# The rare-overflow branch of a mixture-of-experts layer moved from the middle of the layer to its end

## The chip, the cores and the metric

The kernel runs on one core of one Trainium2 chip. The metric is the device time of one execution in microseconds. Three timed runs of the kernel before gave 2019.69, 2011.02 and 2018.78 us, a median of 2018.78 us. One further execution was profiled.

## The reference

The model has 256 tokens of width 1024 and two blocks one after the other, each two layers deep. The change touches the first block alone. Each of its layers is attention (dilated in layer 0, stick-breaking in layer 1), a layer norm, a mixture of experts, and a layer norm again:

```python
scores = jax.nn.sigmoid(xt @ router_w)           # 256 x 16 experts
# per token: the best of 4 groups, in it the 2 best experts, gates that sum to 1
y[t] = sum over the 2 chosen e of gate[t, e] * (silu(x[t] @ w_gate[e]) * (x[t] @ w_up[e])) @ w_down[e]
x = layer_norm(x * DEEPNORM_ALPHA + y, ln2_g, ln2_b)
```

Any expert may in principle be chosen by any number of tokens. Here x @ w_gate and x @ w_up are 1024 to 256 columns, w_down is 256 to 1024 columns.

## The kernel before

The two token halves c = 0, 1 (128 rows each) are the lists x[0], x[1]. The mixture layer is the function moe.

Routing gives each token a rank within each of its experts. For the usual case each of the 16 experts gets 64 slots: P is a 0/1 matrix from tokens to slots, and gather(k, b, t) multiplies 128 columns of x by P on TensorE, in two parts of precision (four products per call). XT holds the gathered columns. A call gather(k, 0, ...) for k = 0 to 7 serves the first eight experts; the first two go to psB, the next six to psA (four buffers). Then up(n) multiplies the slots of a pair of experts with their gate and up weights, hidden and hidden_T make the activation, the down weights follow, and back returns the slots to the tokens. After every two pairs, add adds the sum into x[c] in VectorE; the last two pairs stay in PSUM in acc and are added at the end, after which layer_norm writes y. The second half's layer norm is kept back in self.rest, which the next layer calls (finish).

A slot number above 64 does not fit. For that case there is a branch: ci holds the largest number of tokens of an expert, values_load loads it into a register of all five engines' queues (line 921), and tc.If(rv > 64) (line 922) guards overflow, which computes all 16 experts densely for the tokens that did not fit. Each engine jumps over its own part of the body. A tile that the body reads or writes counts as used by it: whoever needs that buffer next waits for the engine of the body to be past the branch. What is traced behind the branch is issued behind it, and what is traced ahead of it, ahead of it; between two branches the order on each queue is laid out by a planner.

Before, the branch stands in the gather, between gather k = 1 and k = 2. The body writes its transposed x into the buffer of XT, and its weights pass through the ring "row".

Buffers: the ring "x" has four buffers of 128 x 1024 (new_x takes two), the ring "raw" four (weights as loaded, in all layers), XT one. Weights come from SP's queue. In the next layer each weight tile is split: ScalarE copies the high part (whi<-raw, line 240), VectorE subtracts (wlo, line 241). layer_norm first writes the statistics of its input into the first twelve columns of its output y (line 418), then scales and shifts (lines 424, 427). The next layer's first step after layer 0 is the transposition of x[0] (line 266) into xTh and xTl, after layer 1 the squares of the second block's norm (line 294).

Of the kernel before, what the change touches and what calls it, by code (L numbers as in the profile page):

```python
# [7 lines left out]
F32 = mybir.dt.float32  # L8
# [3 lines left out]
OP = mybir.AluOpType  # L12
# [3 lines left out]
ALPHA = float(4 ** 0.25)  # L16
# [153 lines left out]
class Net:  # L170
# [643 lines left out]
    def moe(self, x, l):  # L814


        nc, A = self.nc, self.A
        v, tt, stt, act = nc.vector, nc.vector.tensor_tensor, nc.vector.scalar_tensor_tensor, nc.scalar.activation
        with self.tc.tile_pool(name="moe", bufs=1) as sp, self.psum(512) as self.pa:
# [21 lines left out]

# [78 lines left out]

            rv = nc.values_load(ci[0:1, 0:1], min_val=0, max_val=256)
            with self.tc.If(rv > 64):
                self.overflow(x, l, rank, gt)

# [35 lines left out]
            def add(ns):  # L960
                for c in range(2):
                    acc = [self.psA() for _ in range(2)]
                    back(acc, c, ns, True, True)
                    for s, a in zip(self.halves, acc):
                        stt(out=x[c][:, s], in0=x[c][:, s], scalar=1.0 if ns[0] else ALPHA, in1=a, op0=OP.mult, op1=OP.add)

            p = up(0)
            for n in range(8):
# [26 lines left out]
            y, gb = self.new_x(), self.ln_rows(l, 1)  # L995
            for c in range(2):
                with self.tc.issue_after(self.end.ins) if c else ExitStack():
                    for s, a in zip(self.halves, acc[c]):
                        tt(out=x[c][:, s], in0=x[c][:, s], in1=a, op=OP.add)
                if c == 0:  # L1000
                    self.layer_norm(x[0], gb, y[0], True)
        self.rest = lambda: self.layer_norm(x[1], gb, y[1])
# [15 lines left out]
    def overflow(self, x, l, rank, gt):  # L1018
# [4 lines left out]
        XT = sp.tile([128, 8, 1024], F32, name="XTo", tag="XT")[:, :, :256]  # L1023
        for c in range(2):
            for k in range(0, 8, 4):
                t = self.psC()
                for j in range(4):
                    nc.tensor.transpose(t[:, j * 128:j * 128 + 128], x[c][:, (k + j) * 128:(k + j) * 128 + 128], self.ident)
                self.evac(XT[:, k:k + 4, c * 128:c * 128 + 128], t.rearrange("p (j s) -> p j s", j=4))
        y = self.acc()  # L1030

        def load(ap):
            for j in range(2):
                raw = self.row()
                nc.sync.dma_start(out=raw, in_=ap[:, j * 1024:j * 1024 + 1024])
                yield raw

        for e in range(16):
            p = [self.psC() for _ in range(2)]
            for b in range(2):  # L1040
                for j, w in enumerate(load(self.A["egu"][l, e, b])):
                    for i in range(2):
                        k = 4 * b + 2 * j + i
                        for c in range(2):
                            self.mm(p[c], XT[:, k, c * 128:c * 128 + 128], w[:, i * 512:i * 512 + 512], k == 0, k == 7)
            hs = [self.hidden(p[c], g2[:, c, e:e + 1]) for c in range(2)]
            hs = [self.hidden_T(h) for h in hs]
            for j, w in enumerate(load(self.A["edn"][l, e])):
                for c in range(2):
                    for i in range(2):  # L1050
                        self.mm(y[c][i], hs[c][:, j, :], w[:, self.halves[i]], e == 0 and j == 0, e == 15 and j == 1)
        for c in range(2):
            for s, a in zip(self.halves, y[c]):
                v.scalar_tensor_tensor(out=x[c][:, s], in0=a, scalar=1.0 / ALPHA, in1=x[c][:, s], op0=OP.mult, op1=OP.add)
# [689 lines left out]
```

## Time and profile before

| | us |
|---|---|
| median of three timed runs | 2018.78 |
| lowest, highest | 2011.02, 2019.69 |
| the profiled execution, its own time | 2027.7 |
| its span, first to last instruction | 2025.7 |
| TensorE busy | 1919.8 (95%) |
| VectorE busy | 1186.3 (59%) |
| ScalarE busy | 862.8 (43%) |

Times in the profile count from the start of the span. PE is TensorE's products, PEld its weight loads, DVE VectorE, ACT ScalarE, POOL GpSimd, SP SyncE; a name with q (PEq, SPq) is the queue of that engine. A row gives the work as out<-in by the names of the tiles. Waits stand in brackets: the idle time ahead and what ended it. The mixture layer of layer 0 runs from about 326 to 485 us, that of layer 1 from about 636 to 795 us. [...]

### The profile page before, as it was taken

The numbers are of one execution on the slowest core, as the hardware profiler recorded it, in microseconds if no ns is written. First come the engines' busy times: TensorE is split into PE (matmuls) and PEld (weight loads), VectorE is DVE, ScalarE is ACT, GpSimd is POOL, SyncE is SP. The second block draws the span as 40 slices with busy tenths as digits, with TensorE's granted clock in tenths as the row PEclk, the third lists the DMA queues.
The fourth block names the chain that finished last, engine by engine and source line by source line (L and its number), as shares of the span: only waits on it lengthen the run. The fifth ranks groups of instructions, "written<-read, shape, count | busy, mean of one in ns | idle before, by whom it ended". The sixth has DMA issues, their size and how long they took to land. (4 is left out here: it accounts for less than half of the span.)

```text
span 2025.7 us, 36997 instructions
## 1 busy us (share of the span) xinstructions
PE 1919.8 (95%) x14866; PEld 1622.0 (80%) x14866; DVE 1186.3 (59%) x2329; ACT 862.8 (43%) x1786; POOL 193.3 (10%) x225
## 2 busy tenths in 40 slices
PE   7999997997897997999999999999999999999998
PEld 7999996434885443899888988998999888888997
DVE  6778775125876124855576556555555675556554
ACT  5656552112662112544543335445544533235443
POOL 1323220000220000000021100000000030100000
PEclk9999998998998998999998999999999999899999
DMA  8345346795436796655532215555555532215553
GB/s 280 126 137 164 127 135 240 278 408 191 146 125 222 268 388 232 211 188 187 184 113 77 93 62 178 185 188 168 199 187 188 188 103 83 84 61 176 189 186 107
DMA packets 102516, 357.10 MB, mean 176 GB/s; under 512 B 11888, under 2 KB 15136, under 8 KB 102208
## 3 DMA queue, kind: packets, MB, share of 16 engines
q1 hardware_dynamic: 97584, 341.70, 49.1%
q10 hardware_dynamic: 4704, 12.81, 2.0%
q8 instruction: 120, 1.97, 0.4%
q14 instruction: 60, 0.49, 0.1%
q0 software_dynamic: 48, 0.13, 0.0%
HBM read 353.53 MB, written 1.07 MB: 175 GB/s over the span
## 5 line engine op out<-in xcount | busy, mean ns | idle before, releaser
L241 DVE TENSOR_TENSOR wlo<-raw,whi 128x512 fp32r<-128x512 f32 (+1 forms) x910 | 626.1, 715 | 384.0 <-ACT whi L240 380.1
L240 ACT ACTIVATE whi<-raw 128x512 fp32r<-128x512 f32 (+1 forms) x910 | 529.8, 616 | 592.3 <-issue 197.6
L245 PE MATMUL psB<-xTh,whi 128*128 128x256 f32 x1792 | 507.7, 283 | 12.3 <-ACT whi L240 8.3
L247 PE MATMUL psB<-xTh,wlo 128*128 128x256 f32 x1792 | 506.4, 283 | 0.2 <-DVE wlo L241 0.2
L246 PE MATMUL psB<-xTl,whi 128*128 128x256 f32 x1792 | 506.1, 282 | 0.4
L245 PEld LDWEIGHTS psB<-xTh,whi 128*128 128x128 f32 x1792 | 340.1, 190 | 18.1 <-ACT whi L240 9.8
L246 PEld LDWEIGHTS psB<-xTl,whi 128*128 128x128 f32 x1792 | 340.1, 190 | 5.4 <-DVE xTl L241 1.5
L247 PEld LDWEIGHTS psB<-xTh,wlo 128*128 128x128 f32 x1792 | 340.3, 190 | 1.4 <-DVE wlo L241 0.7
L247 PE MATMUL psA<-whi,hl 128*128 128x512 f32 x352 | 139.5, 396 | 0.0
L245 PE MATMUL psA<-whi,hh 128*128 128x512 f32 x352 | 139.4, 398 | 0.0
L246 PE MATMUL psA<-wlo,hh 128*128 128x512 f32 x352 | 138.7, 394 | 0.0
L245 PE MATMUL psA<-xTh,whi 128*128 128x256 f32 (+1 forms) x352 | 107.8, 307 | 0.3 <-ACT vt L536 0.2
L247 PE MATMUL psA<-xTh,wlo 128*128 128x256 f32 (+1 forms) x352 | 105.1, 299 | 0.0
L246 PE MATMUL psA<-xTl,whi 128*128 128x256 f32 (+1 forms) x352 | 103.6, 295 | 0.3 <-DVE xTl L241 0.3
L245 PE MATMUL psB<-whi,xTh 128*128 128x384 f32 (+2 forms) x256 | 90.3, 353 | 3.6 <-DVE qs L547 1.7
L247 PE MATMUL psB<-whi,xTl 128*128 128x384 f32 (+2 forms) x256 | 88.7, 347 | 0.4 <-DVE xTl L241 0.3
L246 PE MATMUL psB<-wlo,xTh 128*128 128x384 f32 (+2 forms) x256 | 88.5, 346 | 0.3 <-DVE wlo L241 0.3
L296 POOL TENSOR_TENSOR ss<-ss,mh 128x1 f32<-128x1 f32 x14 | 9.8, 702 | 785.5 <-DVE ss L295 780.8
L250 PE MATMUL psB<-raw,XT 128*64 128x512 f32 x288 | 83.5, 601 | 0.0
L247 PEld LDWEIGHTS psA<-whi,hl 128*128 128x128 f32 x352 | 66.0, 188 | 16.8 <-DVE hl L241 0.7
L246 PEld LDWEIGHTS psA<-wlo,hh 128*128 128x128 f32 x352 | 66.6, 189 | 12.6
L245 PEld LDWEIGHTS psA<-whi,hh 128*128 128x128 f32 x352 | 66.3, 188 | 12.8 <-ACT hh L240 0.9
(414 smaller groups left out, 3036.1 us busy)
## 6 DMA issues: line engine op xcount, KB each, us to landing
raw<-in_ffn1gu_dram SPq DMA_DIRECT2D x88, 512.0 KB, 3.8
raw<-in_ffn2gu_dram SPq DMA_DIRECT2D x88, 512.0 KB, 3.7
raw<-in_egu_dram SPq DMA_DIRECT2D x72, 512.0 KB, 9.9
wf<-in_egu_dram SPq DMA_DIRECT2D x56, 512.0 KB, 8.6
raw<-in_dqk_dram SPq DMA_DIRECT2D x46, 512.0 KB, 3.9
raw<-in_ffn1dn_dram SPq DMA_DIRECT2D x44, 512.0 KB, 3.6
raw<-in_ffn2dn_dram SPq DMA_DIRECT2D x44, 512.0 KB, 3.6
raw<-in_wb_dram SPq DMA_DIRECT2D x40, 512.0 KB, 3.7
```

Source lines behind the costliest of these rows:

```text
L240: self.hi = self.nc.scalar.activation(hi, src, AF.Copy)
L241: return (self.nc.gpsimd if pool else self.nc.vector).tensor_tensor(out=lo, in0=src, in1=hi.bitcast(F32), op=OP.subtract)
L245: mm(out, a[0], b[0], start=start, stop=False)
L246: mm(out, a[0], b[1], start=False, stop=False)
L247: mm(out, a[1], b[0], start=False, stop=stop)
L250: return self.nc.tensor.matmul(out, a, b, start=start, stop=stop)
L296: nc.gpsimd.tensor_tensor(out=ss[:, 3:4], in0=ss[:, 2:3], in1=self.mh[:, :1], op=OP.pow)
```

## The change

The branch moves from the gather to the end of the layer, behind the last product and ln_rows, ahead of the last addition. The register load stands behind the first up. Since the body must still read x at the end, the sums go into a new pair of buffers z instead of into x; y is taken behind the branch. The body works on one token half after the other, adds into z, and takes its weights through the ring "raw", twice as many loads as before.

```diff
             t0 = [gather(k, 0, self.psB()) for k in range(2)]
-
-            rv = nc.values_load(ci[0:1, 0:1], min_val=0, max_val=256)
-            with self.tc.If(rv > 64):
-                self.overflow(x, l, rank, gt)
-
             fetch(todo[len(homes):])
             XT = sp.tile([128, 8, 1024], F32, name="XT")
...
                     for s, a in zip(self.halves, acc):
-                        stt(out=x[c][:, s], in0=x[c][:, s], scalar=1.0 if ns[0] else ALPHA, in1=a, op0=OP.mult, op1=OP.add)
-
+                        if ns[0]:
+                            tt(out=z[c][:, s], in0=z[c][:, s], in1=a, op=OP.add)
+                        else:
+                            stt(out=z[c][:, s], in0=x[c][:, s], scalar=ALPHA, in1=a, op0=OP.mult, op1=OP.add)
+
+            z = self.new_x()
             p = up(0)
+            rv = nc.values_load(ci[0:1, 0:1], min_val=0, max_val=256)
             for n in range(8):
...
-            y, gb = self.new_x(), self.ln_rows(l, 1)
+            gb = self.ln_rows(l, 1)
+
+            with self.tc.If(rv > 64):
+                self.overflow(x, z, l, rank, gt)
+            y = self.new_x()
             for c in range(2):
                 with self.tc.issue_after(self.end.ins) if c else ExitStack():
                     for s, a in zip(self.halves, acc[c]):
-                        tt(out=x[c][:, s], in0=x[c][:, s], in1=a, op=OP.add)
+                        tt(out=z[c][:, s], in0=z[c][:, s], in1=a, op=OP.add)
                 if c == 0:
-                    self.layer_norm(x[0], gb, y[0], True)
-        self.rest = lambda: self.layer_norm(x[1], gb, y[1])
+                    self.layer_norm(z[0], gb, y[0], True)
+        self.rest = lambda: self.layer_norm(z[1], gb, y[1])
...
-    def overflow(self, x, l, rank, gt):
+    def overflow(self, x, z, l, rank, gt):
...
-        XT = sp.tile([128, 8, 1024], F32, name="XTo", tag="XT")[:, :, :256]
+        XT = sp.tile([128, 8, 1024], F32, name="XTo", tag="XT")
+        y = [self.psA() for _ in range(2)]
+
+        def load(ap):
+            for j in range(2):
+                raw = self.wp.tile([128, 1024], F32, name="raw", bufs=self.nraw)
+                nc.sync.dma_start(out=raw, in_=ap[:, j * 1024:j * 1024 + 1024])
+                yield raw
+
         for c in range(2):
+            xT = XT[:, :, c * 128:c * 128 + 128]
             for k in range(0, 8, 4):
                 t = self.psC()
                 for j in range(4):
                     nc.tensor.transpose(t[:, j * 128:j * 128 + 128], x[c][:, (k + j) * 128:(k + j) * 128 + 128], self.ident)
...
+            for e in range(16):
+                p = self.psC()
+                for b in range(2):
+                    for j, w in enumerate(load(self.A["egu"][l, e, b])):
+                        for i in range(2):
+                            k = 4 * b + 2 * j + i
+                            self.mm(p, xT[:, k, :], w[:, i * 512:i * 512 + 512], k == 0, k == 7)
+                hT = self.hidden_T(self.hidden(p, g2[:, c, e:e + 1]))
+                for j, w in enumerate(load(self.A["edn"][l, e])):
                     for i in range(2):
...
+                        self.mm(y[i], hT[:, j, :], w[:, self.halves[i]], e == 0 and j == 0, e == 15 and j == 1)
+            for s, a in zip(self.halves, y):
+                v.tensor_tensor(out=z[c][:, s], in0=z[c][:, s], in1=a, op=OP.add)
```

## Rows read from the trace of the kernel before

**Rows 1.** The page, part 1: busy time of an engine, share of the span, instructions.
```profile
PE 1919.8 (95%) x14866; PEld 1622.0 (80%) x14866; DVE 1186.3 (59%) x2329; ACT 862.8 (43%) x1786; POOL 193.3 (10%) x225
```

**Rows 2.** The branch's line, both layers: queue, operation, ns min/median/max; then who waited.
```profile
L922 PEldq COMPARE_BRANCH  x2: 6052/6070/6088, 340.7 to 650.5; - x2
...
L922 DVEq COMPARE_BRANCH  x2: 56/64/72, 342.8 to 652.5; - x2
...
  PE psA L250: 11.9, 2
  ACT XT L536: 10.6, 2
```

**Rows 3.** Timeline of the gather, layer 0: start, us, engine, work, [idle before, releaser].
```profile
340.09 1.05 PE L250 MATMUL psB<-P,xsl 128*128 128x512 f32 x2
...
346.96 0.77 PE L250 MATMUL psA<-P,xsh 128*128 128x512 f32 x1 [5.81 <-PEq L922]
...
354.73 1.94 PE L250 MATMUL psB<-raw,XT 128*64 128x512 f32 x8
```

**Rows 4.** The same, layer 1.
```profile
649.55 1.06 PE L250 MATMUL psB<-P,xsl 128*128 128x512 f32 x2
...
656.74 0.77 PE L250 MATMUL psA<-P,xsh 128*128 128x512 f32 x1 [6.13 <-PEq L922]
...
664.88 1.94 PE L250 MATMUL psB<-raw,XT 128*64 128x512 f32 x8
```

**Rows 5.** Stretches: length, busy time (and count) by engine, granted clock, DMA share, GB/s.
```profile
337.08:341.14 4.06, 4.06 (x8) 2.29 (x8) 3.78 (x9) 0.63 (x1) 0.00 (x0) 0.50 1.02 404
341.14:344.50 3.36, 0.01 (x1) 0.00 (x0) 1.95 (x4) 0.63 (x1) 0.00 (x0) 1.00 1.03 408
346.96:351.34 4.38, 4.38 (x10) 3.44 (x11) 1.28 (x2) 1.20 (x2) 0.00 (x0) 0.50 0.50 180
351.34:354.73 3.39, 3.39 (x15) 2.45 (x14) 0.80 (x2) 1.20 (x2) 0.00 (x0) 1.00 0.22 82
...
650.60:656.74 6.14, 0.01 (x2) 0.04 (x1) 1.95 (x4) 0.63 (x1) 0.00 (x0) 0.50 0.69 272
355.00:370.00 15.00, 15.00 (x80) 8.01 (x76) 1.79 (x5) 1.58 (x3) 0.00 (x0) 1.00 0.60 184
445.00:460.00 15.00, 13.69 (x64) 5.43 (x64) 2.51 (x5) 1.85 (x4) 0.00 (x0) 1.00 1.03 408
```

**Rows 6.** DMA queues from 340.7 to 344.1 us: packets, MB, share.
```profile
q1 hardware_dynamic: 381, 1.39, 102.0%
```

**Rows 7.** DMA queues from 344.1 to 345.4 us.
```profile
q8 instruction: 1, 0.02, 5.3%
```

**Rows 8.** The register load's line, both layers.
```profile
L921 PEldq TENSOR_LOAD <-ci x2: 314/400/487, 340.1 to 650.1; - x2
```

**Rows 9.** Timeline of the end of layer 0.
```profile
472.97 2.89 SPq L221 DMA_DIRECT2D raw<-in_sv_dram  x4
...
484.25 0.39 PE L250 MATMUL psB<-yel,PT 128*128 128x512 f32 x1
...
485.20 1.28 DVE L418 BATCH_NORM_STATS2 x<-x 128x6 f32<-128x512 f32 x2
...
485.70 2.69 ACT L240 ACTIVATE whi<-raw 128x512 fp32r<-128x512 f32 x5
...
489.94 1.94 PE L266 MATMUL psC<-c0t,x 128*128 128x128 f32 x8 [5.30 <-DVE x L427]
...
491.06 0.60 ACT L240 ACTIVATE xTh<-psC 128x512 fp32r<-128x512 f32 x1 [2.67 <-PE psC L266]
```

**Rows 10.** Timeline of the end of layer 1.
```profile
795.86 1.28 DVE L418 BATCH_NORM_STATS2 x<-x 128x6 f32<-128x512 f32 x2
...
800.48 0.63 ACT L294 ACTIVATE row<-x 128x512 f32<-128x512 f32 x1 [3.57 <-DVE x L427]
```

**Rows 11.** DMA issues from 470 to 500 us: KB each, median us to landing.
```profile
raw<-in_sv_dram SPq DMA_DIRECT2D x4, 512.0 KB, 5.8
```

More of the change, by code (lines that the diff above doesn't have):

```diff
@@ L1028, in overflow @@
                     nc.tensor.transpose(t[:, j * 128:j * 128 + 128], x[c][:, (k + j) * 128:(k + j) * 128 + 128], self.ident)
[L1029 to L1041, printed above, removed]
-                    for i in range(2):
[L1043 to L1054, printed above, removed]
+                self.evac(xT[:, k:k + 4, :], t.rearrange("p (j s) -> p j s", j=4))
+            for e in range(16):
[7 more added lines that the diff above has]
+                for j, w in enumerate(load(self.A["edn"][l, e])):
+                    for i in range(2):
+                        self.mm(y[i], hT[:, j, :], w[:, self.halves[i]], e == 0 and j == 0, e == 15 and j == 1)
+            for s, a in zip(self.halves, y):
+                v.tensor_tensor(out=z[c][:, s], in0=z[c][:, s], in1=a, op=OP.add)
     def second_consts(self, pool):
```

## Prediction

> **What bounds the kernel now.** I read the page first. TensorE is busy for 95% of the span [rows 1], so only time in which TensorE stands still, or runs at the lower clock, can be won or lost. Next I read the line of the branch, which runs twice, once a layer. The branch instruction takes 6.07 us on TensorE's queue and 0.06 us on VectorE's [rows 2], and both TensorE's products and ScalarE's copies of XT waited for TensorE's queue to come past it, 11.9 and 10.6 us for the two layers. The timeline of the gather shows the place: the last product before the branch ends at 340.09 + 1.05 = 341.14 us, the next starts at 346.96 [rows 3]; in layer 1 the hole is 6.13 us [rows 4]. [...] Last, the end of the layer: TensorE ends at 484.25 + 0.39 = 484.64 us, then stands for 5.30 us until the normalized x[0] is there to transpose [rows 9]. That is the hole into which the branch moves.
>
> **Removed: the stall in the gather.** The reader is to see that the branch body is not run (nothing of its tiles is in the trace); what costs is TensorE's own jump over it. Without it the 24 products of the six gathers left (k = 2 to 7, four each) follow at once. Their inputs are in time: VectorE's last work before the branch fits into the 1.95 us that it is busy in the stretch behind 341.14 [rows 5], and psA has four buffers. The lower bound of the gain is the hole alone, 5.8 and 6.1 us. The upper bound has all 24 products at the high clock: 24 x 0.23 = 5.5 us, so the first expert product starts at 341.14 + 5.5 = 346.6 instead of 354.73 us, 8.1 us sooner; in layer 1 (hole 650.60 to 656.74, then 664.88 [rows 4]) 656.1, 8.8 us sooner. In layer 0 the clock was already granted at 1.00 when TensorE stopped, after 4.06 us of products, and it fell only behind the idle stretch; in layer 1 it was still at 0.50 [rows 5]. So I take 7.6 near the upper end for layer 0, and 7.4, the middle, for layer 1: **gain 15.0 us** (11.9 to 16.9).
>
> **Moved: the register load.** It stands behind the first expert products now. On TensorE's queue it takes 0.40 us, and from its start (340.1) to the branch (340.7) pass 0.6 us [rows 2, 8]. TensorE's queue runs ahead of the array, so between 0 and 0.6 us a layer; I take 0.3, **loss 0.6 us**. On the other four queues the same load meets idle time. SP and POOL pass the branch too; SP no longer meets it with loads in flight, and its next weight loads had to wait for buffers at either place: nothing. The additions into z are of the size of those into x, on VectorE, which is busy for 1.79 of 15 us between 355 and 370 and for 2.51 of 15 between 445 and 460 [rows 5]: nothing; without that cover it would be tenths of a microsecond a layer. The two loads of ln_rows now stand before the branch on SP, where nothing waits for them until the layer norm.
>
> **Added: the branch at the end.** Here the stall is not simply covered by TensorE's 5.30 us hole, and that is the main step. Two chains start behind TensorE's passing. (1) The branch body reads x[c] with TensorE (transposes), and y = new_x() takes x's buffers, as the ring holds four and z holds two. The first write into y is the statistics of the layer norm, which go into y[:, :12]. So this VectorE instruction, 485.20 us before [rows 9], waits until TensorE is past the branch, as ScalarE's XT copies do now [rows 2]. Behind it stand the whole layer norm, the transposes and the next layer's first product. (2) The body's weights now lie in the raw ring, read by TensorE. The next layer's first four weight tiles, which SP issues at 472.97 us before [rows 9], wait for the same moment.
>
> How long is the jump there? Upper bound: the same instruction, 6.07 us. Lower bound: in the gather the one packet of TensorE's instruction queue does not lie between 340.7 and 344.1 us, where the weight loads fill 102% of the DMA engines [rows 6], but between 344.1 and 345.4 [rows 7], and TensorE goes on at 340.7 + 6.09 = 346.8. If the fetch began at once, 346.8 - 344.1 = 2.7 us would be left. At the end of the layer TensorE's jump meets idle DMA engines, as the weight loads of the next layer wait too. So the row is an upper end, but how much of the first 3.4 us was the load can't be read from it; I take the middle, 4.4 us. [...] The jump is issued some 0.44 us before the last product ends (340.7 against 341.14), so at 484.2 here; it is past at 488.6, and 0.17 us later (346.79 to 346.96) the waiting engine starts: 488.8 against 485.20, **3.6 us a layer, 7.2 us** (1.9 to 5.2 a layer, 3.8 to 10.4). Layer 1 has the same distance, its statistics start at 795.86 [rows 10].
>
> Chain (2) on top. A weight tile lands 5.8 us after its issue by the median [rows 11], the transposed x is ready for ScalarE 491.06 - 485.20 = 5.9 us after the statistics [rows 9]. ScalarE's queue is in order, and before, the eight copies of these tiles (five of them in 2.69 us, 0.54 each) stand ahead of xTh in layer 0 [rows 9], four ahead of the squares at 800.48 us in layer 1 [rows 10]. If none stands ahead any more, nothing is added. If all eight do, with the tiles 1.3 us apart (512 KB at 408 GB/s [rows 5]), xTh starts 5.8 + 3 x 1.3 + 1.1 = 10.8 us after the passing instead of 5.9, 4.9 us more. ScalarE's own loads of constants behind the layer's end (msb, c2t) now land among these tiles, within the same bounds. I take 1.5 a layer, between the ends but nearer the lower, since tile and xTh come due within a microsecond of each other (5.8 against 5.9) and VectorE's work on x[1] can fill what is lost: **3.0 us** (0 to 9.8).
>
> **Sum:** -15.0 + 0.6 + 7.2 + 3.0 = -4.2 us. The profiled execution took 2027.7 us for its span of 2025.7 and would take 2023.5; the three timed runs have a median of 2018.8, 9 us lower, so I forecast 2018.8 - 4.2 = **2014.6 us**. Bounds: -16.9 + 3.8 = -13.1, and -11.9 + 1.2 + 10.4 + 9.8 = +9.5 us.
>
> **Rivals.** (a) The cost at the end nearly vanishes: the jump takes its lower 2.7 us and the copies stand behind xTh: -15.0 + 0.6 + 3.8 = -10.6, 2008.2 us. For it speaks the packet that came only as the weight loads ebbed [rows 6, 7]; against it that layers 0 and 1 show nearly the same 6.09 and 6.05 us. (b) The jump is cheap altogether, as on VectorE, 0.06 us [rows 2], because its target happens to be at hand: TensorE is past before 485.20, only the late weights cost: about -14 us, 2005 us. The body on TensorE is as long as before, which speaks against it. [...] (c) Slower: ScalarE's in-order queue holds xTh behind all late copies, and the jump stays at 6.07: -15.0 + 0.6 + 10.4 + 9.8 = +5.8, 2024.6 us. It decides from 7.2 us a layer on, that is, from 3.6 us of waiting behind the passing. For it speaks the order of before, against it that the copies can be laid out anew, as the code behind the branch is now ordered by itself. (d) The gain is not had: the weight stream sets the end of the layer. From 445 to 460 us the DMA engines are full at 408 GB/s and TensorE is busy for 13.69 of 15 us [rows 5]. Then -0 + 10.8, 2029.6 us. Against it: from 355 to 370 us the DMA engines are busy for only 0.60, because buffers come free as TensorE uses them, so the stream starts sooner with TensorE.
>
> **Chances and range.** The forecast 0.48, (a) 0.25, (b) 0.07, (c) 0.13, (d) 0.07. A measurement tells about 0.5%, 10.1 us, from no change: below 2008.7 or above 2028.9 us. Faster: all of (b), half of (a), a tenth of the forecast, 0.25. Slower: most of (d), a fifth of (c), 0.07. The same: 0.68. The range reaches from (b) to (c), 2005 to 2024 us; the forecast's own is 2009 to 2020.
>
> **What the changed profile would show.** The branch on TensorE at the end of each layer with 3 to 6 us; no hole above 1 us in the gather, and the first expert product about 6 us behind the last product on psB, not 354.73 - 341.14 = 13.6 us. The statistics of the layer norm waiting for TensorE's queue at that line, about 3.6 us later against the last product than now, and the next layer's first raw loads issued right behind it. The prediction is wrong if the statistics start before TensorE is past, if the gather still waits, or if ScalarE stands for more than 4 us on a weight tile with the transposed x ready.

## Result and profile after

The changed kernel takes **2030.6 us** (median of 16 runs, 2020.6 to 2038.4) against 2018.6 us (16 runs, 2010.4 to 2025.4) on the same chip: ratio **1.0062 [1.0046, 1.0079]**, some 12 us slower. The forecast was 2014.6 us, with a range up to 2024.

The page, part 1: TensorE's work is what it was [rows 1].

```profile
PE 1919.0 (95%) x14866; PEld 1621.4 (80%) x14866; DVE 1187.1 (59%) x2329; ACT 862.6 (43%) x1786; POOL 192.9 (10%) x225
```

The branch's line, both layers (it is L996 now), and who waited for it, us in total and times.

```profile
L996 DVEq COMPARE_BRANCH  x2: 63/68/72, 481.8 to 794.4; - x2
L996 PEldq COMPARE_BRANCH  x2: 3539/3609/3679, 482.1 to 794.7; - x2
...
  PE psA L250: 7.8, 2
  DVE x L1002: 2.0, 2
```

The jump is at the end of the layer and lasts 3.5 and 3.7 us, against 6.05 and 6.09 in the gather [rows 2]. Next the timeline of the gather, both layers: the last product on psB and the first expert product.

```profile
341.24 1.06 PE L250 MATMUL psB<-P,xsl 128*128 128x512 f32 x2
...
347.23 1.94 PE L250 MATMUL psB<-raw,XT 128*64 128x512 f32 x8
...
654.68 1.05 PE L250 MATMUL psB<-P,xsl 128*128 128x512 f32 x2
...
660.93 1.94 PE L250 MATMUL psB<-raw,XT 128*64 128x512 f32 x8
```

The hole is gone. From the first gather product to the first expert product pass 10.0 and 10.3 us, 7.7 and 8.1 less than before [rows 3 to 5]: the forecast's 7.6 and 7.4, met. Of these stretches the granted clock tells as well (layer 0, before, then changed: length, busy time and count of PE, PEld, DVE, ACT and POOL, granted clock, DMA share, GB/s; in layer 1 0.58, then 0.72):

```profile
337.08:354.73 17.65, 11.84 (x32) 8.21 (x33) 7.81 (x15) 3.65 (x6) 0.00 (x0) 0.69 0.63 245
```

```profile
337.23:347.23 10.00, 10.00 (x32) 7.65 (x32) 7.54 (x15) 3.66 (x6) 0.00 (x0) 0.74 0.84 333
```

Now the end of layer 0.

```profile
481.73 0.40 PE L250 MATMUL psB<-yel,PT 128*128 128x512 f32 x1
482.60 0.69 DVE L1002 TENSOR_TENSOR x<-x,psA 128x512 f32<-128x512 f32 x1 [0.89 <-DVEq L996]
485.75 2.89 SPq L221 DMA_DIRECT2D raw<-in_sv_dram  x4
485.78 0.77 PE L250 MATMUL psA<-yel,PT 128*128 128x512 f32 x1 [3.65 <-PEq L996]
486.34 0.63 PE L250 MATMUL psB<-yel,PT 128*128 128x512 f32 x1
486.58 0.69 DVE L1002 TENSOR_TENSOR x<-x,psA 128x512 f32<-128x512 f32 x1 [3.30 <-PE psA L250]
...
487.19 1.28 DVE L418 BATCH_NORM_STATS2 x<-x 128x6 f32<-128x512 f32 x2
...
489.79 1.15 ACT L240 ACTIVATE whi<-raw 128x512 fp32r<-128x512 f32 x2 [8.92 <-DMA raw<-in_sv_dram]
...
491.03 1.94 PE L266 MATMUL psC<-c0t,x 128*128 128x128 f32 x8 [4.06 <-ACT whi L240]
...
492.80 0.58 ACT L240 ACTIVATE xTh<-psC 128x512 fp32r<-128x512 f32 x1
...
495.41 0.58 PE L245 MATMUL psB<-whi,xTh 128*128 128x256 f32 x1 [1.38 <-ACT whi L240]
```

Three things stand here. Two of the layer's own last products were laid behind the branch, so they, the second half of the last addition and the statistics wait for the jump; without it they would have ended near 482.6 and the statistics begun 0.56 us later as before [rows 9], at 483.2 instead of 487.19: 4.0 us late (4.5 in layer 1 by the same count). The next layer's loads are issued right behind the jump, at 485.75, not ahead of the last products as before (472.97, [rows 9]). ScalarE then stands for 8.92 us on the first of these tiles, and TensorE's second projection product 1.38 us for a high part. At the end of layer 1, where the 1442 KB of c2t are loaded at the same time, xTh stands behind a tile that is late:

```profile
799.98 1.28 DVE L418 BATCH_NORM_STATS2 x<-x 128x6 f32<-128x512 f32 x2
...
807.22 1.94 PE L266 MATMUL psC<-c0t,row 128*128 128x128 f32 x8 [7.45 <-ACT whi L240]
...
809.30 1.83 ACT L240 ACTIVATE whi<-raw 128x512 fp32r<-128x512 f32 x3 [2.12 <-DMA raw<-in_ffn1gu_dram]
...
811.03 1.06 ACT L240 ACTIVATE xTh<-psC 128x512 fp32r<-128x512 f32 x2
```

All this is the cost at the layer's end that the forecast put at 10.2 us. The surprise is between the two ends of the layer. From the first expert product to the layer's last product, before and then changed:

```profile
354.73:484.64 129.91, 126.57 (x545) 53.80 (x544) 29.62 (x53) 18.69 (x38) 0.00 (x0) 1.00 0.84 316
```

```profile
347.23:486.97 139.74, 131.16 (x545) 55.37 (x544) 30.28 (x53) 17.68 (x36) 0.00 (x0) 0.98 0.76 286
```

The same 545 products take 9.8 us more. Only 4.4 us of these are the jump and the two products behind it (486.97 against 482.6). The other 5.4 us of the 7.7 won in the gather were spent inside the layer, ahead of the branch.

### The profile page after: what moved, and what is told of

Same layout as the page of the kernel before. It is cut to its first block, busy times and chain, and to the rows that moved or that the text cites. A ratio compares the mean times of both kernels' runs of the same rounds, so it can differ in the third digit from the quotient of the medians.

```text
span 2028.8 us, 36976 instructions
## 1 busy us (share of the span) xinstructions
PE 1919.0 (95%) x14866; PEld 1621.4 (80%) x14866; DVE 1187.1 (59%) x2329; ACT 862.6 (43%) x1786; POOL 192.9 (10%) x225
## 4 chain that ended last, share of the span: by engine, by line
PE 53%; DVE 3%; ACT 1%; issue 1%; POOL 1%; DMA 0%; SPq 0%; DVEq 0%; POOLq 0%; ACTq 0%
PE psB L247 8%; PE psB L246 8%; PE psB L245 8%; PE psA L245 7%; PE psA L247 7%; PE psA L246 6%; PE psC L250 5%; PE psB L250 3%; DVE wlo L241 1%; DMA raw<-in_ffn1gu_dram 0%; PE psC L266 0%; DVE row L298 0%; ACT xTh L240 0%; ACT whi L240 0%; DVE xTl L241 0%
## 5 line engine op out<-in xcount | busy, mean ns | idle before, releaser
L245 PE MATMUL psB<-xTh,whi 128*128 128x256 f32 x1792 | 508.7, 284 | 10.8 <-ACT whi L240 8.1
L245 PEld LDWEIGHTS psB<-xTh,whi 128*128 128x128 f32 x1792 | 340.7, 190 | 16.6 <-ACT whi L240 9.0
L247 PEld LDWEIGHTS psA<-whi,hl 128*128 128x128 f32 x352 | 66.1, 188 | 16.3 <-DVE hl L241 0.7
L245 PEld LDWEIGHTS psA<-whi,hh 128*128 128x128 f32 x352 | 66.4, 189 | 12.5 <-ACT hh L240 0.9
```

The source lines that it names most:

```text
L245: mm(out, a[0], b[0], start=start, stop=False)
L247: mm(out, a[1], b[0], start=False, stop=stop)
```

## How to compare the runs

One execution is not enough here. The last 9176 products, from the end of the first feed-forward network (about 1000 us) to the end of the kernel, lie far behind everything that the change touches. They took 1007.0 us in a second profile of the kernel before (first fence) and 1018.6 in the changed kernel (second fence), and by the counts and by the busy times of the other engines they are the same work (length, busy time and count of PE, PEld, DVE, ACT and POOL, granted clock, DMA share, GB/s):

```profile
1000.90:2007.90 1007.00, 980.98 (x9176) 884.02 (x9176) 608.55 (x1224) 449.65 (x947) 71.07 (x100) 0.99 0.43 144
```

```profile
1004.80:2023.40 1018.60, 989.54 (x9176) 892.01 (x9176) 608.83 (x1224) 449.63 (x947) 71.24 (x100) 0.98 0.43 143
```

What differs is how long TensorE was granted half of its full speed (a granted 0.50 and not 1.00; the means are 0.99 and 0.98): PE's busy time grows with the length, by 8.6 us. So beside each median stands the mean over all runs of span times granted clock: the time that the execution would take at a granted 1.00 throughout if all of it went with the clock, "at full clock" below. It counts a microsecond at a granted 0.50 as half of one, waiting included, so it compares kernels and is no time that anyone measured. Its standard error is 0.6 to 1.4 us. It is 1965.2 us for the kernel before (114 runs, standard error 0.3; its medians on the chips used were 2018.6 to 2024.5). Ratios are against runs of the kernel before on the same chip.

| kernel | median us | ratio | clock | at full clock |
|---|---|---|---|---|
| changed | 2030.6 | 1.0062 [1.0046, 1.0079] | 0.9712 | 1970.2 |
| b_none | 2023.5 | 1.0020 [1.0001, 1.0040] | 0.9714 | 1963.8 |
| a_none | 2022.1 | 1.0000 [0.9976, 1.0024] | 0.9733 | 1964.9 |
| a_raw2 | 2025.5 | 1.0016 [0.9996, 1.0035] | 0.9736 | 1968.7 |
| a_pin | 2031.0 | 1.0055 [1.0034, 1.0076] | 0.9714 | 1971.5 |
| a_pin_raw2 | 2017.7 | 0.9977 [0.9955, 0.9999] | 0.9759 | 1968.2 |
| a_hide | 2012.5 | 0.9955 [0.9930, 0.9981] | 0.9769 | 1965.7 |
| a_mid | 2025.4 | 1.0029 [1.0005, 1.0052] | 0.9709 | 1965.3 |
| b_light | 1991.7 | 0.9867 [0.9819, 0.9914] | 0.9745 | 1938.9 |
| b_none_light | 1986.4 | 0.9823 [0.9775, 0.9871] | 0.9745 | 1933.0 |
| b_short | 2009.3 | 0.9938 [0.9915, 0.9962] | 0.9750 | 1958.5 |
| b_reg | 2010.3 | 0.9939 [0.9911, 0.9968] | 0.9738 | 1955.8 |
| b_none_reg | 2002.1 | 0.9921 [0.9893, 0.9949] | 0.9753 | 1952.2 |
| a_reg | 2018.2 | 0.9975 [0.9950, 1.0000] | 0.9731 | 1960.4 |
| a_hide_reg | 2002.9 | 0.9925 [0.9894, 0.9956] | 0.9761 | 1953.7 |

## Experiments

**No branch at all.** From the kernel before and from the changed one the same lines go.

```diff
-            rv = nc.values_load(ci[0:1, 0:1], min_val=0, max_val=256)
-            with self.tc.If(rv > 64):
-                self.overflow(...)
```

> The kernel before without the register load, the branch and the branch's body; all the rest as it was. What the stall at the gather is worth at most. Theory 1 (the expert weights' stream takes the gain back inside the layer): in the changed kernel the first expert product came 7.7 and 8.1 us earlier in the two layers, the last one only 2.1 and 4.6 us; so without any branch the kernel gains some 5 to 9 us and not more: 2010 to 2014 us, and the last expert product of the layers stands 2 to 5 us earlier than before though the first stands some 7 to 8 us earlier. Rival (the gain of the gather is kept and lost at the end of the layer alone): 15 us less, 2003 to 2005 us, with the last expert product 7 us earlier in each layer.

> The changed kernel without the register load, the branch and its body; the sums stay in the new buffers z. What is left of the change when nothing branches. If the other buffers cost nothing, the time is that of the kernel before without a branch, within 2 us. Theory 1 (the weights' stream): 2010 to 2014 us, that is 17 to 21 us less than the changed kernel, all of which the branch at the end of the layer then costs with what hangs on it. Rival (buffers cost): 3 us or more above the kernel before without a branch.

Measured: neither is faster than the kernel before (2023.5 and 2022.1 us). The first expert products come 7 to 9 us earlier, and a stop of 6 us a layer is gone, for nothing. The two agree within 1.1 us at full clock, so no cost of the buffers z shows, and the branch at the end costs the changed kernel 1970.2 - 1964.9 = 5.3 us at full clock, 1.0062 - 1.0000 or 12.5 us in time. This looked like theory 1, the weights' stream.

**Half of the weights' bytes**, with and without the branch (half of each expert weight is left out, the other half used twice).

```diff
-                    raws[e, i] += self.fetch(ap, ring=ring)
+                    raws[e, i] += self.fetch(ap[:, :512], ring=ring)
```

> The kernel before with half of each expert weight left out: of every load of 1024 columns only the first 512 are fetched, and the products use these twice, so instructions and branch stay as they are and the stream's bytes are halved. It is the partner of the next kernel, the same without a branch. Theory 1 (the weights' stream paces the later expert products): the stage from the first to the last expert product is shorter than the 120 us of the kernel before, by 10 to 25 us a layer, and the DMA engines are never full in it. Rival (TensorE's own work paces the stage): no more than 4 us a layer are gained.

> The kernel without a branch, with the same half of each expert weight left out. Theory 1: with the stream out of the way the 7 to 8 us that the first expert product comes earlier are kept to the last expert product, 6 to 8 us a layer, and the time is 12 to 16 us under that of its partner with the branch at the gather. Rival (the lead is lost to something other than the stream, the clock or the order on TensorE): the lead shrinks to 1 to 4 us as with full weights, and the two times differ by under 6 us.

Measured: 5.3 us between the two, 5.9 at full clock. The lead at the first expert product was itself only 5.3 and 5.2 us, since the jump had become shorter (below), and 3.6 and 5.2 us of it reached the layer's last product. At full clock the stage from the first expert product to the layer's last product is 121.2 us in all four layers. The lead is kept here, as theory 1 wants, though the difference of the two times is under 6 us, as its rival wants; and it proved less than it seemed to, since both kernels of this pair have the same order on TensorE, and the pair before had not. Against the kernel before, half of the bytes take 26 us off at full clock; the order on TensorE was laid anew there too, so this is not the stream's price alone.

**A short body.** The jump's target is brought nearer: the body does one expert of sixteen (b_short) or six (b_mid) and leaves out the rest; it is not run with these inputs.

```diff
-        for e in range(16):
+        for e in range(1):
```

> The kernel before with the branch's body cut from sixteen experts to one, 44 products instead of 464 on TensorE; the body is not run with these inputs. If the jump's length comes from the distance to its target, as the forecast took it, it falls from 6.05 us to under 0.3 us, and the hole in the gather to under 1 us; the time is then that of the kernel before without a branch, 2018 to 2025 us, no faster than before. Rival (a taken branch on TensorE always has to fetch while the DMA engines are full): 5 to 6.3 us as before.

> The same with six experts, 184 products on TensorE. If the distance decides, and there is a distance up to which the target is at hand, the jump is either under 0.3 us or 5 to 6.3 us, nothing between. Rival (the jump grows with what is skipped): 2 to 3 us.

Measured, the branch's line in the two:

```profile
L922 PEldq COMPARE_BRANCH  x2: 212/285/358, 338.8 to 648.7; - x2
```

```profile
L922 PEldq COMPARE_BRANCH  x2: 6059/6160/6262, 337.3 to 650.8; - x2
```

Over 44 products the jump takes 0.2 to 0.4 us, over 184 as long as over 464. So it is the far target that costs, and nothing between was seen. The second half of the expectation failed, and that turned the study: the hole shrank only to 2.75 us, since TensorE then waits for VectorE to pass,

```profile
342.00 0.79 PE L250 MATMUL psA<-P,xsh 128*128 128x512 f32 x1 [2.75 <-DVEq L922]
```

yet the kernel is **12.5 us faster** by its ratio (0.9938 [0.9915, 0.9962], four runs; 6.7 us at full clock), against 4 us slower with no branch (1.0020). The stop at the gather is worth something after all. The time from one round's first activation (ScalarE, line 779) to the next in layer 0 shows what differs:

| round after round, us | 1-2 | 2-3 | 3-4 | 4-5 | 5-6 | 6-7 | 7-8 |
|---|---|---|---|---|---|---|---|
| before | 12.0 | 12.3 | 11.4 | 15.9 | 22.0 | 12.5 | 20.1 |
| b_short | 11.9 | 12.3 | 11.4 | 15.9 | 22.0 | 12.5 | 20.1 |
| b_none | 11.9 | 12.3 | 12.5 | 18.6 | 22.4 | 12.8 | 20.1 |
| changed | 11.9 | 12.3 | 12.5 | 17.8 | 22.6 | 12.8 | 20.1 |

In b_short each round comes 2.8 us earlier against the gather and lasts as long; a stream at its limit would not allow that. From the first expert product to the layer's last one, b_short and then b_none:

```profile
350.12:479.99 129.87, 126.53 (x545) 53.77 (x544) 29.65 (x53) 18.67 (x38) 0.00 (x0) 1.00 0.84 316
```

```profile
345.08:481.08 136.00, 130.70 (x545) 54.97 (x544) 29.90 (x53) 17.65 (x36) 0.00 (x0) 0.99 0.83 309
```

The order of b_short's products on TensorE between the first and the last up product is that of the kernel before, instruction by instruction. Without the branch at the gather the tool that lays out the program orders these products anew. TensorE hardly waits for weights there: 0.4 us once in layer 0 of b_none and of the changed kernel, never in their layers 1. In the order as laid it is thus not the stream that lengthens the stage. In b_none's timeline of the fifth round, up products (psB) and down products of the round before (psA) alternate, and the up products end late:

```profile
411.25 0.33 PE L787 MATMUL psC<-c0t,eh 128*128 128x128 f32 x1
...
412.60 1.87 PE L250 MATMUL psB<-wf,XT 128*64 128x512 f32 x6
413.88 0.59 PE L250 MATMUL psA<-raw,ehT 128*64 128x512 f32 x1
...
415.17 1.45 PE L250 MATMUL psB<-wf,XT 128*64 128x512 f32 x5
416.45 2.75 PE L250 MATMUL psA<-raw,ehT 128*64 128x512 f32 x10
```

The order of the changed kernel is new in the same way, but not that of b_none product by product.

**A fixed order.** The down products of a round wait for the last up product of the next; nothing else changes. In the kernel without a branch, in the changed one, in the one with the mended end (a_hide, below), and in the kernel before.

```diff
-                hT = self.hidden_T(h)
-                y = ...; down products
+                with self.tc.issue_after(self.up.ins):   # last up product of round n + 1
+                    hT = self.hidden_T(h)
+                    y = ...; down products
```

> The kernel before without a branch, with the order on TensorE fixed: the down products of a round wait for the last up product of the next. Order theory: the fifth round lasts 16 us again and not 18.7, the last expert product comes 130 to 133 us after the first gather product and not 135 to 137, and the time falls from 2023.5 to 2012 to 2017 us. Rival (the weights' stream): TensorE waits for weights inside the up products instead, the last expert product stays at 135 to 137 us, and the time at 2020 to 2025 us.

> The changed kernel with the same fixed order, everything else as changed. Order theory: 3 to 5 us a layer come back, 2021 to 2025 us; the rest of the loss is the layer's end. Rival (the stream): 2029 to 2032 us as changed.

> The kernel with all three edits at the layer's end, and the fixed order. If both costs of the change are taken away, its gain at the gather is left: order theory 2003 to 2008 us, 0.5 to 0.8% under the kernel before. Rival (the stream): 2011 to 2015 us as without the fixed order.

> The kernel before, branch at the gather, with the fixed order on TensorE. If the order of the kernel before was as good as the fixed one, the time stays within 4 us of the kernel before (2017 to 2025 us), and from the first expert product to the last product of the layer pass 130 to 133 us as before; the whole of the 16 us of the run without a branch is then the gather's. If the fixed order is better by itself, some 6 us or more go (2016 us or less), and the gather's share is smaller by as much.

Measured: 20 us less without a branch (1.0020 to 0.9921), 17.6 us less for the changed kernel (1.0062 to 0.9975), which is then **faster than the kernel before** (0.9975 [0.9950, 1.0000]) by 5 us. That this is near the 4.2 us of the forecast is luck, as the last run shows. The order theory holds, though not on each count: the fifth round of b_none_reg lasts 17.5 us and not 16. The last run, b_reg, corrects the size: the fixed order takes 12.3 us off the kernel before too (0.9939), so it is better than either laid order. It takes 9.4 us at full clock off the kernel before, 9.8 off the changed one and 11.6 off b_none. And b_reg, not the kernel before, is the partner of a_reg in the same order: against it the change still costs 4.6 us at full clock (1960.4 to 1955.8, standard errors 0.9 and 1.4), nearly the 5.0 us of the pair as laid. So a fixed order makes both kernels faster and does not save the change.

From the first expert product to the layer's last product, at full clock: 129.7 to 132.4 us with the order of before (two profiles of the kernel before, one of each short body, eight layers, mean 130.3), 132.9 to 134.3 with the new order (b_none twice and a_none, six layers, mean 133.3): **3.0 us a layer**. In the changed kernel and a_raw2, whose order is the same, it is 2.5 us a layer up to the last up product, ahead of the branch. With the fixed order it is 126.6 and 128.5 us behind the branch at the gather (b_reg), 129.9 and 129.5 without it (b_none_reg), 128.8 and 128.4 with the branch at the mended end (a_hide_reg). Here the stream may take part: b_none_reg, then b_reg, from 400 to 450 us,

```profile
400.00:450.00 50.00, 47.96 (x196) 18.54 (x192) 12.42 (x21) 6.47 (x14) 0.00 (x0) 1.00 1.03 410
```

```profile
400.00:450.00 50.00, 48.85 (x212) 20.13 (x210) 12.55 (x22) 6.66 (x14) 0.00 (x0) 1.00 1.02 400
```

full DMA engines in both; between 380 and 470 us TensorE waits eight times 0.2 us for egu tiles without the branch, five times with it. So in the better order 1 to 2 us a layer of the lead are lost too; that the stream takes them fits, but no run here shows it.

**The end of the layer, piece by piece.** a_raw2: the body's weights in the ring "raw2" in place of "raw". a_pin: the register load behind the last product. a_pin_raw2: both. a_hide: both, and the statistics in a tile of their own.

```diff
-                raw = self.wp.tile([128, 1024], F32, name="raw", bufs=self.nraw)
+                raw = sp.tile([128, 1024], F32, name="raw2", bufs=RAW2)
...
+            with self.tc.issue_after(self.last.ins):     # last product of back
+                rv = nc.values_load(ci[0:1, 0:1], min_val=0, max_val=256)
...
-        st = y[:, :12].rearrange("p (s i) -> p s i", s=2)
+        st = self.sp.tile([128, 2, 6], F32, name="st") if pin else y[:, :12].rearrange("p (s i) -> p s i", s=2)
```

> The changed kernel with one word changed: the branch's body takes its weights into the ring of eight expert weight buffers instead of the ring through which the next layer's weights come. Theory 2 (late weights): in the changed kernel the next layer's first loads were issued at 485.75, right behind TensorE's branch, against 472.97 before, and its first products waited for their high parts; with the body in another ring the loads are issued near 473 again, ScalarE no longer waits 8.9 us on the first weight, and 4 to 6 us of the changed kernel's time go (2024 to 2027 us). Rival (the branch itself and the clock behind it set the time): the loads come earlier, but the first products only by under 0.5 us a layer; 2029 to 2031 us.

> The changed kernel with the register load issued after the last product of the layer, so that the last two products on the low part of the experts' outputs stand ahead of the branch on TensorE and not behind it. Theory 3 (what hurts is that these two products stand behind the branch; the layer norm does not wait for TensorE's jump itself): the first batch statistics come near 483.5 instead of 487.2, 3 to 4 us a layer earlier, and 6 to 8 us go: 2022 to 2025 us. Rival (the forecast's mechanism: the statistics are written into buffers that the body reads, so they wait until TensorE has passed its branch near 485.6): the statistics come 1 to 1.5 us earlier, right behind the branch; 2 to 3 us go: 2027 to 2029 us.

> The changed kernel with two edits: the last two products ahead of the branch, and the body's weights in the expert ring; the layer norm's statistics again written into the buffers that the body reads. Beside the run with all three edits (2012.5 us) it shows what the statistics' wait for TensorE's jump is worth. Forecast's mechanism: the statistics start right behind the jump, 2 to 2.6 us later in each layer than with all three edits, and span times granted clock (which takes the clock's part out) is 3 to 5 us above that run. Rival (the wait is hidden behind the next layer's weights): within 1.5 us of it.

> The changed kernel with three edits: the register load behind the last product of the layer (as in the run that put the last two products ahead of the branch), the body's weights in the expert ring (as in the run that freed the next layer's loads), and the first layer norm's statistics in a small tile of their own, so that nothing up to the scaling waits for TensorE to pass its branch. Theory (the cost at the layer's end is these three waits and nothing else): the statistics start within 1 us of the additions, the next layer's transposes come no later behind the last product than without a branch, and the time is that of the changed kernel without a branch, 2020 to 2024 us. Rival (the jump costs also through the clock or the loading of instructions): 2025 us or more with no wait left at the layer norm.

Measured: a_raw2 gives 9.3 us in time (1.0062 to 1.0016) but only 1.5 at full clock: the weights are early again, and the two products behind the branch remain. a_pin gives nothing (1.0055), which neither theory expected. Its timeline says why:

```profile
477.35 0.40 PE L250 MATMUL psB<-yel,PT 128*128 128x512 f32 x1
...
481.58 3.29 SPq L221 DMA_DIRECT2D raw<-in_sv_dram  x4
481.58 1.29 DVE L418 BATCH_NORM_STATS2 x<-x 128x6 f32<-128x512 f32 x2 [2.54 <-PEq L997]
...
485.73 1.15 ACT L240 ACTIVATE whi<-raw 128x512 fp32r<-128x512 f32 x2 [9.69 <-DMA raw<-in_sv_dram]
```

The statistics wait for TensorE's queue itself, the forecast's mechanism, with the products out of the way; but the loads that are issued at the same moment have become the last to arrive, so what the norm gained was lost on them. With both edits the time falls to 0.9977, with all three to 0.9955; between these two lie 2.5 us at full clock, 1.2 us a layer, between what the two theories expected. In a_hide the statistics no longer wait, and the scaling waits for 0.95 us:

```profile
480.95 1.29 DVE L1003 TENSOR_TENSOR x<-x,psA 128x512 f32<-128x512 f32 x2 [0.89 <-PE psB L250]
482.15 1.28 DVE L418 BATCH_NORM_STATS2 st<-x 128x6 f32<-128x512 f32 x2
...
484.82 1.42 DVE L424 SCALAR_TENSOR_TENSOR x<-x,ss,row 128x512 f32<-128x512 f32 x2 [0.95 <-PEq L997]
```

At full clock a_hide is level with a_none (1965.7 to 1964.9): over the whole kernel the end then costs about nothing. The three waits were not all, though: from the layer's last product to the next stage's first product with weights pass 7.9 and 16.3 us in the two layers, in a_none 6.2 and 9.6. How that is made up behind it is open. That the median of a_hide is 9 us lower is granted clock (0.9769 to 0.9733).

**The branch in the middle of the expert stage**, behind the second partial addition.

```diff
                 if n in (2, 4, 6):
                     add((n - 2, n - 1))
+                if n == 4:
+                    rv = ...; with self.tc.If(rv > 64): self.overflow(x, z, l, rank, gt)
```

> The changed kernel with the branch after the second partial addition, in the fifth of eight rounds of the expert products, where the DMA engines were full; the body takes its weights and its transposed rows from other rings, which are free there. Theory 1 (the weights' stream paces this stretch, TensorE waits there anyway): the jump takes 4 to 6 us of TensorE but the last expert product is no more than 1.5 us later than without a branch, and the time is 2020 to 2025 us. Rival (TensorE, busy 8.4 us of 10 in this stretch, cannot take the stop back): the last expert product is 3 to 5 us later in each layer, 2028 us or more.

Measured: 2025.4 us, just over the upper edge of theory 1. The jump is the longest of all:

```profile
L985 PEldq COMPARE_BRANCH  x2: 6137/6222/6308, 443.9 to 755.8; - x2
```

and SP's queue passes the branch too, at 452.0 us in layer 0; the round's last two loads were issued behind it, at 462.5 us, and TensorE waited 6.5 us for one of them. The time cannot tell the two theories apart.

**Second profiles.**

> The kernel before again, for a second profile, since the first one's time was 2027.7 us and the median of its runs about 2020. If the half-speed stretches of the second block are what varies from one execution to the next, this profile has the same times to within 3 us up to 990 us, and the sum of the half-speed stretches behind 990 us is nearer to 40 than to 58 us, at a time of 2015 to 2022 us.

> The kernel with all three edits again, for a second profile: that of its first run was its longest execution. In span times granted clock it stood level with the kernel before (1966.4 to 1965.6 us), yet its median was 8 us lower, with a mean granted clock of 0.977 to 0.973. Theory (the 8 us are TensorE's clock, and in the second block, whose code is the same): the half-speed stretches behind 990 us sum to under 30 us here, against 58 us in the profile of the kernel before, and the time is 2009 to 2014 us. Rival (they are in the two layers): the stretches between 330 and 990 us sum to 10 us less than in the kernel before.

> The kernel before without a branch again, for a second profile. Theory 1 (the weights' stream takes the lead back): from the layer's first gather to the last expert product the layers take 1 to 5 us less than in the kernel before in this profile too, and 7 to 8 us less from the first gather to the first expert product. Rival (what was seen was the scatter of one execution): the two differences agree.

Measured: 2015.2, 2014.6 and 2019.8 us. The kernel before was 7.0 us slower than in its first profile from the first gather product to the end of the first feed-forward's down products (666.4 to 659.4), where 3 were expected, and 17 us faster behind it; a difference of a few microseconds between two single profiles says nothing here. What holds in both pairs of profiles is the lead at the first expert product (18.3 to 10.5 us in the second) and a layer that is shorter from the first gather product to its end, by 1.2 and 4.0 us in the first pair and by 6.1 and 4.5 in the second, by which b_none should be ahead; its median is not. Behind 990 us TensorE stood at a granted 0.50 for 63 us in the first profile of the kernel before and for 18 in the second, for 27 and 21 in those of a_hide. So the expected time under 30 us came in a_hide, but in the second profile of the kernel before as well: it is no mark of the edit.

## Why the prediction failed

**The step that failed** is "gain 15.0 us", carried from the first expert product into the sum. The lead was there (7.7 and 8.1 us; forecast 7.6 and 7.4), but nothing of it reached the kernel's time: with no branch at all the ratios are 1.0020 and 1.0000. The end, forecast at 10.8 us with the register load, cost 12.5 in time (a_none to changed, with intervals that leave 6 us either way). Two things were left out behind the lead. First, the program behind the gather is laid out anew when the branch goes, and the new order on TensorE costs 3.0 us a layer at full clock; the forecast took the expert stage as a block that only moves. Second, the forecast counted the stop in full, but a part of it lay in time at half speed, and that time did not go away. In the gather TensorE stood at a granted 0.50 for 10.9 and 15.4 us before and for 5.1 and 5.7 after, yet the mean clock of the whole execution did not rise with it (0.973 before; 0.9712 changed, 0.9714 b_none, 0.9733 a_none): it came back elsewhere, a part of it in the expert stage (0.98 for 1.00). Why, no run here tells. At full clock the way from the first gather product to the first expert product fell only from 11.0 to 7.4 us (means over four and two layers), 3.6 a layer.

So at full clock: 2 x 3.6 won, 2 x 3.0 lost in the order, 5.3 paid at the end, +4.1 us in sum, where 5.0 were measured (1970.2 to 1965.2). The lower mean clock (0.9712 to 0.973) makes 3 to 4 us more in time. The last 3 us of the 12 stay open: the runs of the kernel before beside it had a lower median than its other sets (2018.6 us against 2018.7 to 2024.5), and no clock of theirs is on record.

How far the order alone explains it is not settled. With one fixed order on both sides the lead brings 3.6 us at full clock (b_reg to b_none_reg, standard error 1.9) of the 6.0 that the way to the first expert product gives there, and the end takes 8.2 (b_none_reg to a_reg). So the change loses in either order, and only the share of each part differs.

**The other terms stood.** The jump at the end: 3.5 and 3.7 us, within 2.7 to 6.07 (4.4 taken). The statistics: 4.0 and 4.5 us late, forecast 3.6; the mechanism is shown by a_pin, but in the changed kernel itself two products behind the branch did it, which the forecast did not see. The late weights: forecast 1.5 us a layer; the trace shows 2.0 in layer 0 (xTh 0.65 later behind its transposes than before, then 1.38) and 2.1 of waiting in layer 1. The cost of the end in all, with the order held fixed: 0.9975 - 0.9921 = 0.0054, some 11 us, with intervals that leave 8 us either way; forecast 10.8 with the register load. That load does not stand behind the first expert products, as the forecast had it, but directly ahead of the branch (TensorE: 481.49 and 482.08 us); its 0.6 us are the same.

**The rivals.** (d), given 0.07, named the right time (2029.6) and the right term, a gain that is not had; that the time fits to a microsecond is luck, since its cause, the stream, is not what lengthened the stage as laid, and may be at work only in the fixed order. (b), the cheap jump, is what a short body gives; with this body it never came. (c) happened in part: xTh did stand behind late copies, in layer 1 for about 2 us. What the forecast named as signs of error did not occur: the statistics were not early, the gather did not wait, and ScalarE did not stand 4 us on a tile with x ready. The sign that was missing is the length of the stage between.

How far the target lies decides the length of the jump in the gather, though not in proportion: 0.2 to 0.4 us over 44 products, 6.06 to 6.26 over 184, 6.05 and 6.09 over 464 [rows 2]. That the jump waits for the packet on the instruction queue, on which the lower bound of 2.7 us rests, was the author's estimate: no run shows that wait, only the packet inside each long jump (last section), and the shortest of the long jumps took 3.28 us (a_pin). The 0.23 us of a product in the upper bound of the gain are 3.39 us over 15 products at a granted 1.00 [rows 5].

**A version that beats both**, the kernel before and the changed one: the fixed order with the mended end (a_hide_reg), 2002.9 us, 0.9925 [0.9894, 0.9956], level with no branch at all in that order (0.9921). Over the branch left in the gather in that order (b_reg, 0.9939 [0.9911, 0.9968]) no gain is shown: the intervals overlap, and at full clock it is 2.1 us with a standard error of 1.7. What stays open is why the kernels with the mended end were granted more clock than the kernel before (0.976 to 0.977 against 0.973); no run here tells.

## What to carry to other kernels

A branch is also a wall for whatever orders the program (here the new order cost 3.0 us a layer): when one is moved, compare the order of instructions on the bounding engine far from it, before anything is credited to the move. A gain at the start of a stage is a gain only if the stage's own length stays; test it with a kernel in which the order is the same and only the suspected stop is shorter, as the short body did here. Fix the order on both sides before a version is called better than the kernel before: here the order was worth more than the move. A branch late in a stage must not gate the next stage's loads (issued 12.8 us later in the changed kernel), nor the buffers that the norm writes first (2.54 us of waiting in a_pin).

## What the runs showed of the hardware

The same taken branch on TensorE, over the same 464 products in the same place, took 6.05 to 6.09 us in the kernel before, where the DMA engines were full when it began (layer 0 [rows 6]; 102.5% in layer 1, from 650.5 to 654.0 us), and 3.6 us with half the weights' bytes, where they were nearly idle (share 0.03 in the jump):

```profile
L922 PEldq COMPARE_BRANCH  x2: 3592/3608/3625, 339.7 to 633.9; - x2
```

In the middle of the full stream (a_mid, a share of 1.03 from 425 to 452 us) it took 6.1 and 6.3 us, at the layer's end 3.3 to 5.4 (3.5 and 3.7 at a share of 0.04 and 0.03 in the changed kernel, 3.28 and 3.60 in a_pin). So in these runs it was longer where the DMA engines were full; the forecast had this only as a bound. In the traces each long jump has a packet of 16 KB on an instruction queue, q8, which came about 1 us after the jump began with the engines idle (1.0 and 0.9 in the changed kernel) and about 3.5 us after it in the full stream (3.5 in both layers of the kernel before), and the jump ended 1.3 to 1.7 us behind the packet. The two jumps over the short body have none. That the jump waits for the packet fits these times, but no run shows it. The packet in the jump of the changed kernel's layer 0 (from 483.0 to 484.4 us):

```profile
q8 instruction: 1, 0.02, 5.1%
```

And one kernel's executions scatter by 28 us (2010 to 2038 for the kernel before, over six chips), most of it in the time at a granted 0.50: the spans have a standard deviation of 5.6 us, at full clock of 2.8.
